# Loading the first tile of a row-normalizing kernel by even and odd partitions, in two transfers on one queue

## The chip, the core and the metric

The kernel runs on one core of a Trainium2 chip. The metric is the device time in microseconds (us) of one execution. "PE", "DVE", "ACT", "POOL" and "SP" in the profile are TensorE, VectorE, ScalarE, GpSimd and SyncE; SyncE here only issues transfers. HBM is the memory that holds the input and the output; SBUF is the core's own memory, which holds the tiles. A "span" is the profiled execution without its launch, about 1.7 us shorter than the time. "Packet records" are the start, length and size of every DMA packet in the packed trace; they name neither engine nor partition, so rows are told apart by their order in time alone.

## The reference

```python
batch, dim = 1024, 4096                      # x: float32
norm = np.sqrt(np.sum(x ** 2, axis=-1, keepdims=True) + eps)
return (x / norm).astype(np.float32)
```

It reads 16.8 MB and writes 16.8 MB.

## The kernel before

There are two tiles. Each has 128 partitions with 4 rows of 4096 floats, so that a partition is one contiguous 65,536 bytes in memory and on the core. I call those 65,536 bytes a *row of a tile* from here on.

```python
R = 4
n_tiles = N // (P * R)                                   # 2
x_t = x.rearrange("(t p r) d -> t p (r d)", p=P, r=R)
io = ctx.enter_context(tc.tile_pool(name="io", bufs=n_tiles))   # both tiles fit
# ... (pools, eps, scratch)
groups = []
for i in range(n_tiles):
    g = RowGroups(nc, io, stats, scratch, D, R, eps_t)
    nc.sync.dma_start(out=g.flat(), in_=x_t[i])          # load 0, load 1
    groups.append(g)

for i, g in enumerate(groups):
    g.square_dve(R - 1)        # VectorE: square, accumulate
    g.square_act(0)            # ScalarE: the same for another row
    g.norm(0)                  # ScalarE sqrt, VectorE reciprocal
    g.scale(0)                 # VectorE: multiply in place
    # ... (rows 1, 3 and 2 likewise)
    nc.sync.dma_start(out=out_t[i], in_=g.flat())        # store 0, store 1
```

## Time and profile before

| What | Value | Where it is read |
|---|---|---|
| time | 83.74 us median (83.50 to 83.83, 6 runs) | the runs |
| span | 82.2 us | the profile page |
| VectorE, ScalarE busy | 35%, 32% | the page, busy time |
| share of the 16 DMA engines that is busy | 95.6% | the page, queues |
| tile 0 lands, store 0 is issued | 22.58 us, 38.55 us | timeline |
| tile 1 lands, store 1 is issued | 42.73 us, about 58.1 us | timeline |

How to read it: two compute engines that are idle for two thirds of the time and a DMA share near 1 say that the transfers fill the span. The lines themselves are in the prediction.

### The profile page before, as it was taken

The page shows a single profiled execution, that of the slowest core. Times are in us where ns is not written, and L with a number is a line of the kernel's source. Part 1 is how long each engine was busy: PE and PEld are TensorE (multiplying, and loading weights), DVE is VectorE, ACT ScalarE, POOL GpSimd, SP SyncE. Part 2 cuts the span into 40 slices and gives each one's busy share as a digit, 9 for nine tenths or more (in the row PEclk, how much of TensorE's full clock was granted, in tenths as well). Part 3 has the DMA queues.
Part 4 walks back from the last instruction along what each step waited for, and adds up shares of the span by engine and source line. Part 5 has one row for each costly group of instructions (what it writes and reads, how often), then busy time and mean ns, then how long its engine had stood idle before and what let it go on. Part 6 is the DMA issues. An engine that isn't in the chain of part 4 may idle for free.

```text
span 82.2 us, 93 instructions
## 1 busy us (share of the span) xinstructions
DVE 28.6 (35%) x21; ACT 26.4 (32%) x22; POOL 0.2 (0%) x4
## 2 busy tenths in 40 slices
DVE  0000000000099599977029995999200000000000
ACT  6000000000099999940029999950000000000000
POOL 0000000000000000000000000000000000000000
DMA  9299974999995699999199997599999669999920
GB/s 415 96 510 510 510 319 191 510 510 510 510 510 223 287 510 510 510 510 447 64 510 510 510 447 319 255 510 510 510 478 478 287 287 510 510 510 478 415 128 0
DMA packets 576, 33.55 MB, mean 408 GB/s; under 512 B 64, under 2 KB 64, under 8 KB 64
## 3 DMA queue, kind: packets, MB, share of 16 engines
q1 hardware_dynamic: 576, 33.55, 95.6%
HBM read 16.78 MB, written 16.78 MB: 408 GB/s over the span
## 4 chain that ended last, share of the span: by engine, by line
DMA 51%; ACT 9%; DVE 9%; SPq 0%; issue 0%
DMA xt<-in_x_dram 51%; ACT sq_act L33 9%; DVE xt L64 9%; ACT rstd L53 1%; SPq L106 0%; DVE rstd L59 0%
## 5 line engine op out<-in xcount | busy, mean ns | idle before, releaser
L33 ACT ACTIVATE sq_act<-xt 128x4096 f32<-128x4096 f32 x6 | 21.6, 3608 | 27.4 <-DMA xt<-in_x_dram 27.4
L64 DVE TENSOR_SCALAR xt<-xt,rstd 128x4096 f32<-128x4096 f32 x8 | 18.8, 2353 | 0.3
L42 DVE SCALAR_TENSOR_TENSOR sq_dve<-xt 128x4096 f32<-128x4096 f32 x2 | 8.8, 4424 | 25.9 <-DMA xt<-in_x_dram 25.9
L53 ACT ACTIVATE rstd<-ssq,eps_t 128x1 f32<-128x1 f32 x8 | 2.1, 288 | 0.1
L59 DVE RECIPROCAL rstd<-rstd 128x1 f32<-128x1 f32 x8 | 1.3, 159 | 2.4 <-ACT rstd L53 2.4
L33 ACT ACT_TABLE_LOAD x1 | 1.3, 1283 | 0.7 <-PEq L139 0.7
L53 ACT ACT_TABLE_LOAD x1 | 1.3, 1283 | 0.0
L33 ACT ACTIVATION_READ_ACCUMULATOR sq_act<-xt 128x1 f32 x6 | 1.1, 185 | 0.0
L98 DVE MEMSET eps_t<- 128x1 f32 x1 | 0.1, 59 | 0.8 <-PEq L139 0.8
L42 DVE DVE_READ_ACCUMULATOR sq_dve<-xt 128x1 f32 x2 | 0.2, 81 | 0.0
L139 POOL MEMSET const-uint8-127<- 128x1 uint8 x1 | 0.1, 103 | 0.0
L139 POOL MEMSET const-bfloat16-1.0<- 128x1 bf16 x1 | 0.1, 102 | 0.0
L139 POOL MEMSET const-float32-0.0<- 128x1 f32 x1 | 0.1, 99 | 0.2 <-issue 0.2
L139 POOL MEMSET const-float32-1.0<- 128x1 f32 x1 | 0.1, 99 | 0.0
## 6 DMA issues: line engine op xcount, KB each, us to landing
xt<-in_x_dram SPq DMA_DIRECT2D x2, 31.7
out_dram<-xt SPq DMA_DIRECT2D x2, 23.4
```

The costliest lines, as they stand in the source:

```text
L33: self.nc.scalar.activation(out=sq_a, in_=self.x[:, r], func=ACT_F.Square, accum_out=self.ssq[:, r : r + 1],)
L42: self.nc.vector.scalar_tensor_tensor(out=sq_v, in0=self.x[:, r], scalar=1.0, in1=self.x[:, r], op0=ALU.mult, op1=ALU.mult, accum_out=self ...
L53: self.nc.scalar.activation(out=self.rstd[:, r : r + n], in_=self.ssq[:, r : r + n], func=ACT_F.Sqrt, bias=self.eps_t,)
L59: self.nc.vector.reciprocal(out=self.rstd[:, r : r + n], in_=self.rstd[:, r : r + n])
L64: self.nc.vector.tensor_scalar_mul(out=self.x[:, r], in0=self.x[:, r], scalar1=self.rstd[:, r : r + 1])
L98: nc.vector.memset(eps_t, eps)
L139: nc = _bacc.Bacc("TRN2", target_bir_lowering=False, num_devices=1)
```

## The change

Its intent is to bring the first tile in as two transfers, one for the even and one for the odd partitions, both issued by SyncE.

```diff
+def load_by_parity(dst, src, queues):
+
+    for odd, queue in enumerate(queues):
+        queue.dma_start(out=dst[odd::2], in_=src[odd::2])
 ...
-        nc.sync.dma_start(out=g.flat(), in_=x_t[i])
+        if i == 0:
+            load_by_parity(g.flat(), x_t[i], (nc.sync, nc.sync))
+        else:
+            nc.sync.dma_start(out=g.flat(), in_=x_t[i])
```

## The prediction

Passages of the recorded texts that rest on what no trace or run of this case shows are cut, and the cuts are marked. In the prediction they take the grounds of step 4 away, not its term: the sum on record is 83.76 + 0 + 0.01 + 0 + 14 = 98 us. What is cut held that in the parity load two engines at a time would slow each other (the "pair" in what is left), so that the eight rows of tile 0 would go at half rate, 19.4 us more, and that uneven shares would leave about 14 us of it. The half rate and the 14 us are my estimates; no trace showed a half rate when they were made.

> **What bounds the kernel now.** I read the page's slices first, because they tell in one look whether engines or transfers fill the span; then the queue and the issues; then the stages; then the order of instructions around the two loads and the two stores.
>
> The 40 slices and the queue (a slice is 82.2 / 40 = 2.06 us; digits are busy tenths):
>
> ```profile
> DVE  0000000000099599977029995999200000000000
> ACT  6000000000099999940029999950000000000000
> DMA  9299974999995699999199997599999669999920
> DMA packets 576, 33.55 MB, mean 408 GB/s; under 512 B 64, under 2 KB 64, under 8 KB 64
> q1 hardware_dynamic: 576, 33.55, 95.6%
> ```
>
> VectorE and ScalarE are idle for most of the span; the DMA row is filled to the last slice but one. Of the 576 packets, 64 are the tiny completion packets (4 transfers x 16 engines). That leaves 512 of 33.55 MB / 512 = 65,536 bytes: one packet is one whole partition row of 4 x 4096 floats, 8 rows per DMA engine and transfer. The mean time of a row is 0.956 x 16 x 82.2 us / 512 = 2.46 us. (The packet records under this line say the same: nearly all last 2.418 to 2.422 us, 27.1 GB/s per engine; only the first of each engine, about 3.1 us, and the one before the loads turn into stores, about 2.9 us, are longer. Chained end to start, they form 16 tracks with no gap above some 30 ns.)
>
> The stages (columns: stretch, its length, busy time of DVE, ACT and POOL with instruction counts, clock, DMA share, GB/s):
>
> ```profile
> 2.00:22.00 20.00, 0.00 (x0) 0.01 (x1) 0.00 (x0) 1.00 0.96 413
> 22.00:42.00 20.00, 14.32 (x10) 13.26 (x11) 0.00 (x0) 1.00 1.01 429
> 42.00:61.00 19.00, 14.23 (x10) 11.87 (x10) 0.00 (x0) 1.00 0.97 421
> 61.00:80.00 19.00, 0.00 (x0) 0.00 (x0) 0.00 (x0) 1.00 0.95 414
> ```
>
> Load 0, load 1, store 0 and store 1 follow each other at the same 413 to 429 GB/s; compute on one tile lies beside a transfer of the other. So the page's chain, which gives 51% to the loads and the rest to ScalarE and VectorE, names a chain that just happens to be the last; it isn't what sets the end. The timeline shows how close the two are:
>
> ```profile
> 0.73 0.86 SPq L106 DMA_DIRECT2D xt<-in_x_dram  x2
> ...
> 22.58 4.42 DVE L42 SCALAR_TENSOR_TENSOR sq_dve<-xt 128x4096 f32<-128x4096 f32 x1 [21.72 <-DMA xt<-in_x_dram]
> ...
> 36.16 2.35 DVE L64 TENSOR_SCALAR xt<-xt,rstd 128x4096 f32<-128x4096 f32 x1
> 38.55 19.88 SPq L122 DMA_DIRECT2D out_dram<-xt  x2
> 42.73 3.62 ACT L33 ACTIVATE sq_act<-xt 128x4096 f32<-128x4096 f32 x1 [6.80 <-DMA xt<-in_x_dram]
> ```
>
> Tile 0 lands at 22.58, is done at 38.51, and store 0 is issued at 38.55, while load 1 ends only near 42: some 3 us in hand. Tile 1 lands at 42.73, is done at 58.05 (15.3 us), and store 0 fills the engines until about 61: again some 3 us. The end is thus start (about 2 us) + 32 rows per engine x 2.42 us = 77.4 + the slower few rows and the last completion (about 2.5 us) = 82 us. Whatever lengthens a row of a load moves the end by the same time; whatever only makes a tile land earlier moves nothing.
>
> [...]
> [...]
> [...]
> [...]
> [...]
>
> **The change, part by part.** It removes one issue of 8 rows per engine and adds two of 4 rows. Bytes, row size (65,536), rows per engine (8) and the queue stay.
>
> 1. One more issue on SyncE. Two take 0.86 us together, so one is 0.43 us. The second half is issued while the first one's rows run (4 x 2.42 = 9.7 us). Load 1's issue moves from 1.2 to about 1.6 us, some 18 us before its engines need it. Off the path: 0.
> 2. 16 more completion packets. At the seam of load 0 and load 1 in the packet records, the next row starts within some 10 ns. On the path: about 0.01 us.
> 3. One more semaphore for the first instructions of tile 0 and for store 0. The even half lands early, but every instruction reads all 128 partitions, so none starts before the odd half: gain 0.
> 4. Which engine writes which partition when. This is where I had to choose. [...] The eight rows of tile 0 would go at half rate: 8 x 2.42 = 19.4 us more if both engines of a pair get equal shares and stay in step. [...] I take about 14.
>
> Sum: 83.76 + 0 + 0.01 + 0 + 14 = 98 us. All stages after the load shift with it, with their 3 us in hand kept, because load 1, both computations and both stores are unchanged.
>
> **The rivals.**
> - *Nothing happens.* [...] For it: the same bytes in the same rows, and a page that shows every engine at its own even pace. [...] Time: 83.8 us.
> - *Full lockstep.* The pairs share evenly all the way: 83.76 + 19.4 = 103.1 us. For it: the 16 engines start within 0.7 us and keep their order for the whole run. [...]
> - *Faster, because half a tile is there earlier.* Against: no instruction works on half the partitions, and the transfers are already back to back. It could win a few tenths if the first slow row became shorter: 83.5 us.
> - *The issue becomes the bound.* 3 x 0.43 = 1.3 us before load 1, against 19 us of work queued ahead of it: it can't.
>
> **Range and chances.** I give the clash about two in three[...]. If it comes, [...]it is slower by far over 2%; if not, the time is within 0.2 us of before. Faster than 82.1 us has no mechanism: 0.01. Within 2%: 0.32. Slower: 0.67. The range must hold both outcomes: 83.5 to 103.5 us. I put the point at 98, in the clash and short of full lockstep, since a middle between the two outcomes would describe neither.
>
> **What would show it.** Right: the rows of tile 0 last clearly longer than 2.42 us (up to 4.84) while all later rows keep 2.42; the GB/s of the first 20 us fall to 210 to 290; tile 0 lands at 31 to 42 us instead of 22.6, and every later event is late by the same time; compute durations stay. Wrong on step 4: tile 0 lands at 22.6, and the DMA row looks as before. Wrong on steps 1 to 3: load 1's rows start late with engines idle, or an instruction of tile 0 starts before both halves have landed. If tile 0 is late but the end isn't, my reading that the transfers bound the whole span is wrong.

## The result, and the profile after

The changed kernel takes 83.69 us (median of 6 runs, 83.55 to 83.75), the kernel before 83.74 us in the same rounds. The ratio is 0.9996, with a 95% interval of 0.998 to 1.0011: the same. (Ratios are the mean time of one kernel's fast runs over that of the other's of the same rounds, so not quite the ratio of the medians quoted.) The prediction said 98 us, with 0.67 on slower.

The slices, the packets and the queue of the changed kernel, to be held against those shown of before:

```profile
DVE  0000000000079449997639995999100000000000
ACT  0000000000079999993039999940000000000000
DMA  0999749999958999975999975999994899998490
DMA packets 592, 33.55 MB, mean 409 GB/s; under 512 B 80, under 2 KB 80, under 8 KB 80
q1 hardware_dynamic: 592, 33.55, 95.4%
```

There are 16 more packets, and all of them are tiny: one more transfer with 16 completions (in the packet records packets of 4 bytes, 16 to a transfer, each at the end of one of its last rows). The number of data packets is the same 592 - 80 = 512.

The stages of the changed kernel (columns as in the prediction):

```profile
2.00:22.00 20.00, 0.00 (x0) 0.00 (x0) 0.00 (x0) 1.00 1.00 419
22.00:42.00 20.00, 14.32 (x10) 14.54 (x12) 0.00 (x0) 1.00 1.08 465
42.00:61.00 19.00, 14.23 (x10) 11.87 (x10) 0.00 (x0) 1.00 0.93 404
61.00:80.00 19.00, 0.00 (x0) 0.00 (x0) 0.00 (x0) 1.00 1.00 431
```

The first stage moves 419 GB/s against 413 before. So the two half transfers run at full rate. The packet records say the same row by row: the first row of each engine takes 3.07 us on average (3.11 before), and the seven others of tile 0 take 2.415 to 2.422 us. (A stage counts a packet where it starts, which is why a share can exceed 1.)

The timeline around the loads and store 0 of the changed kernel:

```profile
0.72 1.18 SPq L72 DMA_DIRECT2D xt<-in_x_dram  x2
1.96 0.58 SPq L115 DMA_DIRECT2D xt<-in_x_dram  x1
23.06 1.28 ACT L33 ACT_TABLE_LOAD   x1 [23.06 <-DMA xt<-in_x_dram]
24.35 3.62 ACT L33 ACTIVATE sq_act<-xt 128x4096 f32<-128x4096 f32 x1
...
40.32 17.73 SPq L131 DMA_DIRECT2D out_dram<-xt  x2
42.36 3.62 ACT L33 ACTIVATE sq_act<-xt 128x4096 f32<-128x4096 f32 x1 [4.65 <-DMA xt<-in_x_dram]
```

Two things did move. Tile 0 lands 0.5 us later (23.06 instead of 22.58 us). And ScalarE's table load (ACT_TABLE_LOAD, which the traces show before its first Square and before its first square root) now stands behind a wait for tile 0 and takes its 1.28 us after the landing. In the kernel before it stood at the start:

```profile
0.73 1.28 ACT L33 ACT_TABLE_LOAD   x1 [0.73 <-PEq L139]
```

The likely reason is that ScalarE's first Square now has two transfers to wait for, and the wait for one of them sits on the table load. The runs agree: in every kernel here that loads tile 0 in two or more transfers and has no early Square, the table load stands behind the landing (it starts at 22.90 to 77.75 us), and in every one that loads it in a single transfer it starts by 1.32 us. Together the two put store 0 off by 1.77 us, from 38.55 to 40.32 us.

Yet tile 1 lands at 42.36 us, not later than before (42.73), and the end doesn't move. The packet records show what evens it out: in the kernel before the last rows of load 1 take 2.86 us on average, with store 0 issued as they start; in the changed kernel, where store 0 comes later, they take 2.42 us.

### The profile page after: what moved, and what is told of

Read it like the earlier page. It is cut to its first block, busy times and chain, and to the rows that moved or that the text cites. A ratio compares the mean times of both kernels' runs of the same rounds, so it can differ in the third digit from the quotient of the medians.

```text
span 82.0 us, 96 instructions
## 1 busy us (share of the span) xinstructions
DVE 28.6 (35%) x21; ACT 26.4 (32%) x22; POOL 0.2 (0%) x4
## 4 chain that ended last, share of the span: by engine, by line
DMA 49%; ACT 10%; DVE 9%; SPq 1%; issue 0%
DMA xt<-in_x_dram 49%; ACT sq_act L33 9%; DVE xt L64 9%; SPq L72 1%; ACT rstd L53 1%; DVE rstd L59 0%
```

## The experiments

The prediction failed at step 4, the half rate of tile 0's rows. Two explanations are open at once: either the partitions that are written at the same time don't matter for the rate, or they do, and the parity load (the one by even and odd partitions) is spared a clash, that is, rows that slow each other. And one reading of before, that the transfers bound the whole span, has not been tested, since nothing was slowed.

### Do the partitions of a transfer set its rate? Halves, eighths and every eighth partition

In the halves run tile 0 is loaded as partitions 0-63 and 64-127 (the diffs from here on are shortened to the lines that matter):

```diff
-        queue.dma_start(out=dst[odd::2], in_=src[odd::2])
+        queue.dma_start(out=dst[k * n : (k + 1) * n], in_=src[k * n : (k + 1) * n])   # n = 64
```

In these expectations P is the theory that they do, N that they don't.

> Tile 0 is loaded as partitions 0-63, then 64-127. Theory P[...] each of its 4 rows per engine lasts about 4.84 us instead of 2.42, and those of the second half too; tile 0 lands near 42 us, the time is about 103 us. Theory N (an engine's own rate is the limit[...]): all rows 2.42 us, first half lands near 13 us, tile 0 near 23 us, time 83.7 us. Theory D ([...]the first half to 8 engines only, the second to the other 8): 8 rows of 2.42 us on each engine as before, but both halves land near 22.5 us; time 83.7 us.

Measured: 104.40 us against 83.85 us, ratio 1.245 (1.243 to 1.247). The stages of the halves run:

```profile
2.00:22.00 20.00, 0.00 (x0) 0.00 (x0) 0.00 (x0) 1.00 1.01 210
22.00:42.00 20.00, 0.00 (x0) 0.00 (x0) 0.00 (x0) 1.00 1.02 210
```

The DMA engines are as busy as ever (share 1.01), but move half as much: they are slow, not idle. That is what the share of busy time hides. Most rows of tile 0 take 5.12 us in the packet records; the fifth, the first one of the second half, takes 4.95. The sum comes out: six rows of 5.12 - 2.42, one of 4.95 - 2.42 and a first row of 4.8 instead of 3.1 make 16.2 + 2.5 + 1.7 = 20.4 us; the time rose by 20.55 us. This is what theory P foretold; N and D (each half on eight engines only) foretold 83.7 us and fall.

In the eighths run the same edit has eight transfers of 16 neighbouring partitions each (n = 16):

> Tile 0 is loaded in eight transfers of 16 neighbouring partitions[...]. Theory P: [...]a row lasts about 4 x 2.42 = 9.7 us, tile 0 lands near 80 us, time about 141 us. Theory N: rows 2.42 us, tile 0 lands near 23 us, time 83.5 to 84.5 us; eight issues of about 0.56 us (4.5 us) are hidden since a row takes 2.42. Theory D (few engines per transfer): 4 of the 16 engines with 4 rows each, time between.

Measured: 138.38 us, ratio 1.651 (1.648 to 1.653). Its first stages:

```profile
2.00:22.00 20.00, 0.00 (x0) 0.00 (x0) 0.00 (x0) 1.00 1.09 125
22.00:42.00 20.00, 0.00 (x0) 0.00 (x0) 0.00 (x0) 1.00 0.93 105
```

After the first, rows of tile 0 take 9.28 to 9.30 us, nearly four times 2.42, which is what theory P foretold (9.7).

In the third run the eight transfers take every eighth partition:

```diff
-        queue.dma_start(out=dst[odd::2], in_=src[odd::2])
+        queue.dma_start(out=dst[k::8], in_=src[k::8])        # k = 0 to 7
```

> Tile 0 is loaded in eight transfers of every 8th partition (16 rows each, one per engine). [...] Theory P: rows about 4.84 us, tile 0 lands near 42 us, time about 103 us. Theory N: rows 2.42 us, tile 0 near 23 us, time 83.5 to 84.5 us.

Measured: 104.71 us, ratio 1.249 (1.247 to 1.251), most rows 5.10 us, and in the first stage half the rate:

```profile
2.00:22.00 20.00, 0.00 (x0) 0.00 (x0) 0.00 (x0) 1.00 1.03 213
```

So a strided split is not harmless as such: this one moves 213 GB/s, like the halves (210), where the one by even and odd moves 419.

### The change four times over

```diff
-        if i == 0:
+        if True:
             load_by_parity(g.flat(), x_t[i], (nc.sync, nc.sync))
 ...
-        nc.sync.dma_start(out=out_t[i], in_=g.flat())
+        load_by_parity(out_t[i], g.flat(), (nc.sync, nc.sync))
```

> Both loads and both stores are split by parity: four times the change. Whatever the split costs on the transfers' path shows four times. Theories N and P both: 83.5 to 84.2 us, rows 2.42 us in all stages; four more issues of about 0.5 us beside transfers. If there were a small cost of each split (a completion packet, a seam) it would show as up to 0.2 us for each, so up to 84.5 us.

Measured: 83.78 us, ratio 0.9992 (0.998 to 1.001). Three more splits and 48 more completion packets than in the changed kernel cost nothing that shows, in loads or in stores: the lower and upper ends of the interval are 0.2 us below and 0.06 us above the kernel before.

### Destination or source? Halves fed from parity rows, and the reverse

Up to here the partition and the place in memory went together, so the clash could lie in memory. These two kernels take them apart; both give a wrong result, since the rows of tile 0 are permuted. The first outcome in each expectation is for a clash at the destination in SBUF, the second for one at the source in HBM.

```diff
-        queue.dma_start(out=dst[odd::2], in_=src[odd::2])
+        queue.dma_start(out=dst[64 * odd : 64 * odd + 64], in_=src[odd::2])   # first run
+        queue.dma_start(out=dst[odd::2], in_=src[64 * odd : 64 * odd + 64])   # second run
```

> Wrong result on purpose (rows of tile 0 permuted): the destination is halves of the partitions (0-63, then 64-127), as in the halves run, but the source rows are the even and then the odd ones, as in the changed kernel. [...] time about 104.4 us, rows of tile 0 5.1 us. If it lies at the source in HBM (neighbouring rows read together): 83.7 us, rows 2.42 us.

> Wrong result on purpose (rows of tile 0 permuted): the destination is the even and then the odd partitions, as in the changed kernel, the source rows are 0-63 and then 64-127. [...] 83.7 us, rows 2.42 us. HBM: 104.4 us, rows 5.1 us.

Measured: 104.44 us (ratio 1.246) for the first and 83.72 us (ratio 0.9985) for the second. The first stage of the first run:

```profile
2.00:22.00 20.00, 0.00 (x0) 0.00 (x0) 0.00 (x0) 1.00 1.02 213
```

and of the second run:

```profile
2.00:22.00 20.00, 0.00 (x0) 0.00 (x0) 0.00 (x0) 1.00 1.00 419
```

In the four kernels the time follows the destination alone (104.40 and 104.44 us with halves, 83.69 and 83.72 us with parity): the clash lies on the SBUF side, and the order of rows in memory shows no part in it.

### Is the parity load written like the whole one? A probe at four neighbouring partitions

A probe loads four neighbouring partitions of tile 1, on ScalarE's queue, beside the load of tile 0; load 1 waits for it and writes the same data over it. These three lines replace the two loads in the kernel's loop.

```diff
+    nc.scalar.dma_start(out=groups[1].flat()[92:96], in_=x_t[1][92:96])
+    load_by_parity(groups[0].flat(), x_t[0], (nc.sync, nc.sync))
+    nc.sync.dma_start(out=groups[1].flat(), in_=x_t[1])
```

The expectations of the probes were reckoned from my guesses at which engine writes which partition (N2 and A are two of them). No trace shows that.

> The parity kernel, with a probe: a small transfer of partitions 92-95 of tile 1 (four rows of 65,536 bytes[...]) is issued on ScalarE at the same time; load 1 waits for it and overwrites it. [...] In all theories the 4 engines that carry the probe[...] have slow rows of their own. Theory N2[...]: besides the 4 probe engines exactly one engine has slow rows, and its first ones are slow from the start. Theory A[...]: two engines have slow rows, two each, not the same two in time or only the third and fourth. The time is not of interest (load 1 waits for the probe, some 12 to 20 us, so it may be unchanged).

Measured: 93.55 us. Neither picture came. All sixteen first rows were slow (8.5 to 10.8 us), the four of the probe and all twelve others; the second ones took 2.4 to 4.4 us, and from the third on it was 2.42 us again. So slow rows don't mark single engines: beside the probe the first rows of all sixteen were held up. (No probe with its rows farther apart was run, so how much of this comes from the second queue as such isn't shown; that the probe's place matters is shown by the next runs.) The undisturbed parity load, with rows of 2.42 us, shows nothing of the kind. The probe had to be read in another way, by how long the hold-up lasts: by the end of the last first row, counted from the first packet, and by the time.

The same probe on the kernel before, with the load of tile 0 whole:

> The probe on the kernel before: partitions 92-95 of tile 1[...] on ScalarE beside the unsplit load of tile 0. In the parity kernel the four probe rows and all first rows of tile 0 took 9 to 10.8 us[...]. If the unsplit load deals its rows like the parity load[...]: the same picture, first rows 9 to 11 us, time about 93.5 us. [...]

The parity kernel with the probe at partitions 0-3:

> The parity kernel with the probe at partitions 0-3[...] instead. [...] four rows' time, first rows 9 to 11 us, time 93.5 us. [...] five rows' time, first rows about 12 us, time about 96 us. If two such engines are there at the start[...] about 12 us, for half of the rows.

Measured: 93.58 us and 91.96 us. With the probe at partitions 92-95 the unsplit load takes as long as the parity load (93.58 and 93.55 us), and with the probe at 0-3 the parity load is quicker by 1.6 us. Its last first row ends at 9.6 us instead of 11.8 us, a difference of about one row's time (2.2 us beside 2.42). (In the eighths run, without a probe, it ends at 9.54 us; the next expectation says 9.6.) Three runs follow from this: the control, the unsplit load with the probe at 0-3, and two more places under the parity load.

> Control: the kernel before with the probe[...]. The parity kernel's probes ended their first rows at 11.8 us[...] and 9.6 us[...]; the eighths run[...] at 9.6 us.[...] If the unsplit load is dealt like the parity load[...]: 9.6 us, time about 92 us. If not: 11.8 us, time about 93.5 us.

> The parity kernel with the probe at partitions 4-7[...]. Dealt by partition number, [...] first rows end at 9.6 us, time about 92 us. Dealt four in a run with turns[...] 11.8 us, about 93.5 us.

> The parity kernel with the probe at partitions 24-27[...]. Dealt by partition number, [...] first rows end at 11.8 us, time about 93.5 us. Dealt four in a run with turns[...] 9.6 us, about 92 us.

All six, with the end of the last first row counted from the first packet:

| Load of tile 0 | Probe at partitions | Last first row ends | Time |
|---|---|---|---|
| by parity | 0-3 | 9.6 us | 91.96 us |
| by parity | 4-7 | 9.9 us | 91.79 us |
| by parity | 24-27 | 11.7 us | 93.73 us |
| by parity | 92-95 | 11.8 us | 93.55 us |
| whole | 0-3 | 10.1 us | 91.95 us |
| whole | 92-95 | 11.7 us | 93.58 us |

The start of ScalarE's first Square, which waits for tile 0, shows it in the timeline of the parity kernel with the probe at partitions 4-7:

```profile
32.63 3.62 ACT L33 ACTIVATE sq_act<-xt 128x4096 f32<-128x4096 f32 x1
```

and at 24-27:

```profile
34.48 3.62 ACT L33 ACTIVATE sq_act<-xt 128x4096 f32<-128x4096 f32 x1
```

There are two levels, 91.79 to 91.96 us and 93.55 to 93.73 us, and the probe's place decides between them: at both places that were probed under both loads, parity and whole agree (91.96 and 91.95 us at 0-3, 93.55 and 93.58 us at 92-95). So the probes find no difference between the parity load and the whole one. In each of the last two expectations the outcome named first came (9.9 and 11.7 us); the guess behind it may be right, but isn't shown. What makes the two levels no run shows; my reading of them rested on a dealing of rows that no trace shows, and is left out. A rival would be that partitions 24-27 and 92-95 are slower in themselves. The eighths run shows no such thing among its second to eighth transfers, which hold these two places (9.28 to 9.30 us a row); but partitions 0-7 are in its first one, whose rows are the first of the run and no measure, so the rival stays open. Nor does a run show why the halves clash and the even and odd partitions don't.

### Reads of SBUF: one store by halves

```diff
-        nc.sync.dma_start(out=out_t[i], in_=g.flat())
+            for k in range(2):                                    # store 1 only; store 0 stays whole
+                nc.sync.dma_start(out=out_t[i][64 * k : 64 * k + 64], in_=g.flat()[64 * k : 64 * k + 64])
```

> The kernel before with store 1 alone in halves of the partitions (0-63, 64-127); the loads are whole. [...] rows of store 1 about 5.1 us, 8 x 2.7 = 21.6 us more, time about 105 us. If only writes clash: 83.8 us, rows 2.42 us.

Measured: 103.11 us against 83.98 us, ratio 1.229 (1.226 to 1.232). Its last stage, with store 1:

```profile
61.00:101.30 40.30, 0.00 (x0) 0.00 (x0) 0.00 (x0) 1.00 0.89 190
```

Of the 128 rows of store 1, 86 take 5.1 us. So a store by halves clashes too, where the stores by parity cost nothing that shows (83.78 us). For the store no run took SBUF and HBM apart, so that the clash lies in reading SBUF is inferred from the loads.

### Do the transfers bound the span? Store 0 delayed

```diff
         g.scale(2)
+        if i == 0:
+            for _ in range(2):
+                nc.vector.tensor_scalar_mul(out=g.x[:, 2], in0=g.x[:, 2], scalar1=1.0)
```

The same edit was made in the kernel before, in the changed kernel, and in the changed kernel with an early Square of one column that loads ScalarE's table in advance.

> The kernel before, with two extra multiplications by 1 (2.35 us each, 4.7 us) between tile 0's last scale and store 0. If the transfers bound the whole span, and the slack before store 0 ends where the changed kernel's store 0 is issued (40.3 us, there with gaps of 0.15 us on average): store 0 is issued at 38.55 + 4.7 = 43.25 us, about 3 us too late, time 83.8 + 3.0 = 86.8 us. If the chain of loads and computation on tile 1 sets the end: tile 1 starts at most 0.5 us later, time 83.8 to 84.4 us.

> The changed kernel with the same 4.7 us. If the change has used up 1.8 us of slack without showing it (store 0 at 40.32 instead of 38.55 us): store 0 at 45.0 us, time 83.7 + 4.8 = 88.5 us, 1.7 us more than the same delay on the kernel before. If the change costs nothing anywhere: the same time as the kernel before with the delay.

> The changed kernel with the delay, and with a Square of one column before everything, so that ScalarE's table is loaded while the transfer runs. If the 1.8 us are the table load that had moved behind the wait for tile 0 (1.28 us) and a later landing (0.5 us): 1.28 us come back, time about 87.2 us, table load near 1 us in the timeline. If the slack went elsewhere: 88.5 us as without it.

Measured: 86.03, 87.64 and 87.06 us, against 83.81 us of the kernel before. The issues of the stores in the kernel before with the delay:

```profile
43.27 14.53 SPq L125 DMA_DIRECT2D out_dram<-xt  x2
```

in the changed kernel with the delay:

```profile
45.03 14.52 SPq L134 DMA_DIRECT2D out_dram<-xt  x2
```

and in the changed kernel with the delay and the early table:

```profile
44.36 14.52 SPq L136 DMA_DIRECT2D out_dram<-xt  x2
```

Take from each issue what the run lost: 43.27 - 2.22 = 41.05, 45.03 - 3.83 = 41.20 and 44.36 - 3.25 = 41.11 us. The three agree on one deadline: store 0 must be issued by about 41.1 us. From there on a later issue costs nearly its full lateness: from the first to the second of these runs the issue is 1.76 us later and the time 1.61 us longer. Between the last row of load 1 and the first of store 0 the packet records show mean gaps of 2.8, 4.1 and 3.6 us per engine, where the undelayed kernels have 0.0 and 0.15. The rival, that tile 1's load and computation set the end, is out: in the kernel before with the delay tile 1 landed no later,

```profile
41.97 3.62 ACT L33 ACTIVATE sq_act<-xt 128x4096 f32<-128x4096 f32 x1 [5.97 <-DMA xt<-in_x_dram]
```

store 1 was issued at 57.5 us (before 58.1), no later either, and the time still grew.

The slack was thus 41.1 - 38.55 = 2.5 us before and 41.1 - 40.32 = 0.8 us after. The expected times were 0.8 us too high for the first two, since I had set the deadline at 40.3 us. Their difference of 1.6 us is the 1.7 expected: the change does cost something, inside the slack. The early table gave back 0.6 us of the 1.3 expected. Its Square on tile 0 starts 1.34 us earlier, but the built program then has the square roots in another order, and tile 0 is done only 0.67 us earlier.

## Why the prediction was wrong

- **What bounds the kernel: right.** The delayed stores show it, with 2.5 us in hand where the prediction read "some 3 us".
- **Step 1 (issues): right in effect.** The issues took 0.56 us each rather than 0.43, and load 1 was issued at 1.96 us, far ahead of its need.
- **Step 2 (completion packets): right.** With four splits they still can't be seen in the time (83.78 us against 83.85).
- **Step 3 (waits): right that no gain comes, incomplete in its cost.** It didn't see that the table load would move behind the landing. Store 0 comes 1.77 us later for this and for the later landing. It was hidden because 2.5 us were in hand, not because it was nothing; that these 2.5 us suffice was no part of step 3's reasoning, and so luck.
- **Step 4 (which engine writes which partition when): the step that failed.** It put the rows of tile 0 at half rate. For contiguous halves the rate did halve: rows of 5.12 us where step 4 had 4.84. For the parity transfer it doesn't hold: rows take 2.42 us as in the unsplit load, and under the probes the two loads agree. A clash is real and its size was nearly right (full lockstep 103.1 us foretold, 104.4 us measured for halves), but it isn't in this change. The term of the sum that should have been 0 was the 14 us.
- **The rival that came true** is "nothing happens": 83.8 us foretold, 83.69 us measured. Of its two explanations, one was that writes can't slow each other at all; the halves (rows of 5.12 us) and the eighths (9.28 to 9.30 us) show that they do.
- **Range:** its low end of 83.5 us was put there for that rival, and 83.69 us lies inside. But the point and the odds went with an assumption about who writes which partition that the profile of before couldn't support: its packet records name neither engine nor partition.

The argument against that rival was where I went astray: it went from 64 neighbouring partitions to 64 even ones. The runs show how little the one says of the other: 210 GB/s for the neighbouring ones, 419 GB/s for the even and odd ones.

## What to carry to other kernels

Before a transfer is split, ask which partitions each piece covers, and measure the rows of the pieces. Here even and odd partitions ran at full rate (419 GB/s, whole 413), while neighbouring halves and every eighth partition ran at half rate (210 and 213 GB/s) and moved the end by about 20 us, and sixteen neighbours at a time moved 105 to 125 GB/s. Even and odd, with rows of 65,536 bytes, is the only split at full rate that was found. A DMA share near 1 doesn't tell full speed from a clash (1.00 at 419 GB/s, 1.01 at 210); look at GB/s beside it. And an unchanged time can hide a cost in slack: this change spent 1.8 of 2.5 us, which showed as 1.6 us as soon as a delay of 4.7 us used up the rest.
